# Moving transformed row-block pairs in the feed-forward, one more such pair in each head's gate and value product, and two subtractions written as one

## The chip, the cores and the metric

The kernel runs on one core of a Trainium2 chip. The metric is the device time in microseconds (us) of one execution. The kernel before has a median of 2198.53 us over three executions (2196.38 to 2199.3). A further execution was taken with the hardware profiler; every row of the profile below comes from that one.

## The reference, cut to what is computed

One layer with a sequence of 256 rows, a model width of 2048, 8 retention heads (key width 256, value width 512) and a feed-forward width of 5632. All inputs are float32.

```
h = rms_norm(x, g_mix[i])
proj = h @ w_in[i]
cb, cc, cv, q, k, v, g, gate_conv, gate_ret = jnp.split(proj, split_points, axis=-1)

y_conv = short_conv_mixer(cb, cc, cv, conv_w[i]) @ w_conv_out[i]
...
o = retention(q, k, v.reshape(bsz, s, RET_HEADS, RET_DV))
o = head_group_norm(o, g_ret[i], x.dtype)
y_ret = (jax.nn.silu(g) * o) @ w_ret_out[i]

merged = jax.nn.sigmoid(gate_conv) * y_conv + jax.nn.sigmoid(gate_ret) * y_ret
x = x + merged @ w_o[i]

h = rms_norm(x, g_ffn[i])
a, b = jnp.split(h @ w_ffn_in[i], 2, axis=-1)
x = x + (jax.nn.silu(a) * b) @ w_ffn_out[i]

ple_gate = jax.nn.sigmoid(rms_norm(x, g_ple[i]) @ w_ple_gate[i])
x = x + ple_gate * (p[i] @ w_ple_proj[i])
return rms_norm(x, g_final)
```

The change touches three kinds of product in it: the columns of `h @ w_in` that hold `g` and `v` of one head, the other double column blocks of `h @ w_in`, and `h @ w_ffn_in`.

## The kernel before

**How a product is formed.** Activations lie transposed in the on-chip memory, in blocks of 128 rows of the inner dimension, and weights stream in from HBM. Every float32 operand is used as two parts, hi (the value rounded to the matmul's input type) and lo (what is left of it). One block product is therefore three matmuls of 128x512: hi by hi, hi by lo, lo by hi. The function `thrice` issues them, and they are L230, L231 and L232 in the profile. For weights ScalarE (ACT) makes hi with a cast (L350) and VectorE (DVE) makes lo with a subtraction (L351); the matmul by a lo part cannot start before DVE has written it.

**Groups and places.** The function `product_group` multiplies the 256 rows by two weight blocks of 512 columns side by side, over an inner dimension of 16 row blocks. It takes the row blocks two at a time; these eight pairs are called places 0 to 7 here. A pair is a 2x2 block product (two row halves of the activations, two row blocks, two column blocks). A *plain* pair does it with 8 block products, 24 matmuls. A *transformed* pair uses the Winograd form of Strassen's scheme: 7 block products, 21 matmuls, and for it sums of weight blocks and sums of activation blocks. In the names, `b` is a weight block as loaded, `t` a weight sum, `h2T_s` or `hF_s` an activation sum and `h2T_d` or `hF_d` an activation difference, which plain pairs ahead of the last transformed one use.

**What a pair costs on the other engines.** A plain pair needs one ACT cast and one DVE subtraction of 128x2048. A transformed pair needs on DVE: the lo part of three weight blocks (128x1536, L351), four sums or differences of 128x512 in place in the raw tile (L278, L279, L281, L282), and the lo parts of the four sums (two of 128x1024, L285); on ACT a cast of 128x1536 (L350) and two of 128x1024 (L280, L283). The hi and lo parts come from one pool of 6 tiles (`part`): a plain pair takes 2 of them, a transformed pair 4. Raw weights have 3 tiles, which two loads of 512 KB each fill by SyncE's queue.

**The stages.** First the norm and head 0; then heads 1 to 7, each with a projection of q and k (`qk`), a gate and value group (`gv1` to `gv7`, a `product_group`) and the retention itself, and the output projection of the heads (`ro`) in between; then the convolution (groups `cv0` to `cv3`, `cb0`, `cb2`), the gates (groups `gate0` to `gate3`), `wo`, the feed-forward, the embedding gate and the final norm. The feed-forward runs over 11 groups `f0` to `f10`. Each ends with a sigmoid and four products on DVE (L830, L833) that give `f_ca`. After f2 to f9 come four chunks of 24 matmuls each of the product with `w_ffn_out` (`fo`, L370 to L372), two row block chunks for each of two column blocks; after f10 come the last twelve. The result of a group has to be transposed for that: `turn_a` does it with 8 small matmuls on TensorE (`aT`, L147).

**Which places are transformed.** In `gv`, `cv` and `cb` groups and in f0 and f1 places 1 and 3; in the gates places 1, 3 and 5; in f2 to f10 places 1, 3, 4 and 6.

**What sets the order.** Engines run their instructions in the order of their queues, which a scheduler fixes when the program is built. Work that must wait for other engines is put off by hand: `later(n, fn)` runs `fn` after n more groups, where a call of `group_done` after each pair or chunk counts one.

Of the kernel before, what the change touches and what calls it, by code (L numbers as in the profile page):

```python
# [950 lines left out]
```

## Time and profile before

| what | before |
|---|---|
| median of three executions | 2198.53 us (2196.38 to 2199.3) |
| the profiled execution | 2199.96 us, of which the span from first to last instruction is 2198.2 us |
| mean granted TensorE clock | 0.997 of full speed |
| TensorE, matmuls (PE) | busy 2169.9 us, 99% of the span, 9826 instructions |
| TensorE, weight loads (PEld, beside PE) | busy 1787.4 us, 81% |
| VectorE (DVE) | busy 1651.3 us, 75%, 1692 instructions |
| ScalarE (ACT) | busy 1062.8 us, 48%, 967 instructions |

A busy share is the part of the span in which the engine had an instruction in it. Matmuls overlap: a row gives about 0.39 us for one of 128x512, while in a run without waits a new one starts every 0.23 us. So the distance between starts, and not the duration in a row, is what a matmul takes from the time. In rows of the timeline "x2" is two equal instructions in a row, and the bracket at the end is the idle time of the engine just before, with the instruction that ended it.

### The profile page before, as it was taken

The numbers are of one execution on the slowest core, as the hardware profiler recorded it, in microseconds if no ns is written. First come the engines' busy times: TensorE is split into PE (matmuls) and PEld (weight loads), VectorE is DVE, ScalarE is ACT, GpSimd is POOL, SyncE is SP. The second block draws the span as 40 slices with busy tenths as digits, with TensorE's granted clock in tenths as the row PEclk, the third lists the DMA queues.
The fourth block names the chain that finished last, engine by engine and source line by source line (L and its number), as shares of the span: only waits on it lengthen the run. The fifth ranks groups of instructions, "written<-read, shape, count | busy, mean of one in ns | idle before, by whom it ended". The sixth has DMA issues, their size and how long they took to land.

```text
span 2198.2 us, 25135 instructions
## 1 busy us (share of the span) xinstructions
PE 2169.9 (99%) x9826; PEld 1787.4 (81%) x9826; DVE 1651.3 (75%) x1692; ACT 1062.8 (48%) x967; POOL 9.4 (0%) x19
## 2 busy tenths in 40 slices
PE   8999999999999999999999999999999999999998
PEld 7888888888888888888878888778777878777887
DVE  6687877467785468888987556888888888888555
ACT  6454544444544345555554345544545444445544
POOL 0000000000000000000000000000000000000000
PEclk9999999999999999999999999999999999999999
DMA  7555556655656665455657565456565555556553
GB/s 262 176 195 181 168 176 212 212 173 195 211 177 212 223 215 188 163 182 191 245 183 243 191 206 179 171 190 203 195 217 192 182 181 192 198 204 215 173 196 130
DMA packets 236024, 428.49 MB, mean 195 GB/s; under 512 B 12289, under 2 KB 47233, under 8 KB 235905
## 3 DMA queue, kind: packets, MB, share of 16 engines
q1 hardware_dynamic: 235904, 426.89, 57.8%
q8 instruction: 77, 1.26, 0.2%
q14 instruction: 43, 0.34, 0.0%
HBM read 420.54 MB, written 6.29 MB: 194 GB/s over the span
## 4 chain that ended last, share of the span: by engine, by line
PE 92%; DVE 4%; ACT 2%; issue 1%; DMA 1%; SPq 0%; ACTq 0%; POOLq 0%; DVEq 0%
PE f_p L231 6%; PE f_p L232 6%; PE f_p L230 6%; PE gv_p L230 4%; PE gv_p L231 4%; PE gv_p L232 4%; PE fo_ps L370 3%; PE fo_ps L372 3%; PE fo_ps L371 3%; PE qk_ps L372 3%; PE qk_ps L370 3%; PE qk_ps L371 3%; PE ro_ps L232 3%; PE ro_ps L230 3%; PE ro_ps L231 3%; PE cv_p L231 2%
## 5 line engine op out<-in xcount | busy, mean ns | idle before, releaser
L351 DVE TENSOR_TENSOR f_b_lo<-f_raw,f_b_hi 128x2048 fp32r<-128x2048 f32 (+1 forms) x88 | 179.2, 2046 | 66.7 <-ACT f_b_hi L350 66.7
L350 ACT CAST f_b_hi<-f_raw 128x2048 fp32r<-128x2048 f32 (+1 forms) x88 | 150.6, 1714 | 90.8 <-PE fo_ps L371 39.9
L231 PE MATMUL f_p<-f_b_lo,h2T_hi 128*128 128x512 f32 x402 | 157.1, 391 | 0.5 <-DVE f_b_lo L351 0.5
L232 PE MATMUL f_p<-f_b_hi,h2T_lo 128*128 128x512 f32 x402 | 156.5, 390 | 0.0
L350 ACT CAST gv_b_hi<-gv_raw 128x2048 fp32r<-128x2048 f32 (+1 forms) x56 | 101.0, 1805 | 101.6 <-PE qk_ps L371 45.4
L230 PE MATMUL f_p<-f_b_hi,h2T_hi 128*128 128x512 f32 x402 | 144.6, 393 | 4.1 <-ACT f_b_hi L350 4.1
L351 DVE TENSOR_TENSOR gv_b_lo<-gv_raw,gv_b_hi 128x2048 fp32r<-128x2048 f32 (+1 forms) x56 | 120.1, 2154 | 34.6 <-ACT gv_b_hi L350 34.6
L351 DVE TENSOR_TENSOR ro_lo<-ro_raw,ro_hi 128x2048 fp32r<-128x2048 f32 x32 | 73.4, 2293 | 88.5 <-ACT ro_hi L350 88.5
L371 PE MATMUL fo_ps<-fo_lo,aT_hi 128*128 128x512 f32 x352 | 137.9, 392 | 0.0
L370 PE MATMUL fo_ps<-fo_hi,aT_hi 128*128 128x512 f32 x352 | 137.1, 394 | 0.0
L372 PE MATMUL fo_ps<-fo_hi,aT_lo 128*128 128x512 f32 x352 | 137.0, 390 | 0.0
L231 PE MATMUL gv_p<-gv_b_lo,hT_hi 128*128 128x512 f32 x336 | 131.0, 390 | 0.0
L232 PE MATMUL gv_p<-gv_b_hi,hT_lo 128*128 128x512 f32 x336 | 130.8, 389 | 0.0
L230 PE MATMUL gv_p<-gv_b_hi,hT_hi 128*128 128x512 f32 x336 | 126.8, 393 | 0.0
L350 ACT CAST fo_hi<-fo_raw 128x2048 fp32r<-128x2048 f32 x44 | 84.2, 1914 | 69.1 <-PE fo_ps L371 38.8
L351 DVE TENSOR_TENSOR qk_lo<-qk_raw,qk_hi 128x2048 fp32r<-128x2048 f32 x32 | 73.3, 2291 | 58.5 <-ACT qk_hi L350 58.5
L280 ACT CAST f_t_hi<-f_raw 128x1024 fp32r<-128x1024 f32 x40 | 42.1, 1054 | 145.3 <-DVE f_raw L279 64.1
L351 DVE TENSOR_TENSOR fo_lo<-fo_raw,fo_hi 128x2048 fp32r<-128x2048 f32 x44 | 100.6, 2286 | 14.8 <-ACT fo_hi L350 14.8
L350 ACT CAST ro_hi<-ro_raw 128x2048 fp32r<-128x2048 f32 x32 | 61.2, 1912 | 99.5 <-PE ro_ps L231 65.8
L285 DVE TENSOR_TENSOR f_t_lo<-f_raw,f_t_hi 128x1024 fp32r<-128x1024 f32 x80 | 96.7, 1221 | 16.1 <-ACT f_t_hi L283 8.9
L371 PE MATMUL qk_ps<-qk_lo,hT_hi 128*128 128x512 f32 x256 | 100.3, 392 | 0.0
L372 PE MATMUL qk_ps<-qk_hi,hT_lo 128*128 128x512 f32 x256 | 99.8, 390 | 0.0
(459 smaller groups left out, 5751.0 us busy)
## 6 DMA issues: line engine op xcount, KB each, us to landing
f_raw<-in_w_ffn_in_dram SPq DMA_DIRECT2D x176, 512.0 KB, 4.5
gv_raw<-in_w_in_dram SPq DMA_DIRECT2D x112, 512.0 KB, 4.6
fo_raw<-in_w_ffn_out_dram SPq DMA_DIRECT2D x44, 1024.0 KB, 5.2
qk_raw<-in_w_in_dram SPq DMA_DIRECT2D x64, 512.0 KB, 4.6
ro_raw<-in_w_ret_out_dram SPq DMA_DIRECT2D x64, 512.0 KB, 4.7
cv_raw<-in_w_in_dram SPq DMA_DIRECT2D x64, 512.0 KB, 4.6
gate_raw<-in_w_in_dram SPq DMA_DIRECT2D x64, 512.0 KB, 4.8
cb_raw<-in_w_in_dram SPq DMA_DIRECT2D x32, 512.0 KB, 4.6
```

Source lines behind the costliest of these rows:

```text
L230: nc.tensor.matmul(out=ps, lhsT=xh, rhs=wh, start=first, stop=False)
L231: nc.tensor.matmul(out=ps, lhsT=xh, rhs=wl, start=False, stop=False)
L232: nc.tensor.matmul(out=ps, lhsT=xl, rhs=wh, start=False, stop=last)
L280: nc.scalar.copy(out=hi[:, 0:2, :], in_=raw[:, 0:2, :])
L285: tt(out=lo[:, js, :], in0=raw[:, js, :], in1=hi[:, js, :].bitcast(F32), op=ALU.subtract)
L350: last_copy[0] = nc.scalar.copy(out=hi[:, :n, :], in_=src)
L351: nc.vector.tensor_tensor(out=lo[:, :n, :], in0=src, in1=hi[:, :n, :].bitcast(F32), op=ALU.subtract)
L370: nc.tensor.matmul(out=ps, lhsT=xh[:, ts], rhs=wh, start=first, stop=False)
L371: nc.tensor.matmul(out=ps, lhsT=xh[:, ts], rhs=wl, start=False, stop=False)
L372: nc.tensor.matmul(out=ps, lhsT=xl[:, ts], rhs=wh, start=False, stop=last)
```

## The change

It does four things. The places become an argument: a tuple of the transformed places, and a string of forms by which the activation sums (S), differences (D) or nothing (-) are prepared.

1. Each of the seven groups `gv1` to `gv7` has a third transformed pair, at place 5.
2. In the feed-forward the transformed places are 0, 2, 4, 6 in f2 to f10 (before 1, 3, 4, 6), and 0, 2 in f0 and f1 (before 1, 3). The number of them stays.
3. In every transformed pair the two subtractions L278 and L279, each of 128x512, become one instruction of 128x2x512 (L284 in the kernel after), whose output rows are in reverse order and whose second operand is one block read twice.
4. `turn_a` is put off by three groups and not two, for all but the last group.

The groups `cv`, `cb` and `gate` keep their places. The arguments `k0` and `order` keep their defaults.

```
-FAST3 = (False, True, False, True, False, True, False, False)
-FAST2 = (False, True, False, True, False, False, False, False)
-FAST4 = (False, True, False, True, True, False, True, False)
+FORMS_MIX, FORMS_FFN = "DSDSDS--", "SDSDSDS-"
...
-    def product_group(lhs, forms, fast, w, c1, c2, name):
+    def product_group(lhs, forms, fast, w, c1, c2, name, k0=0, order=range(8)):
-        last_fast = max(i for i, f in enumerate(fast) if f)
+        last_fast = max(at for at, i in enumerate(order) if i in fast)
...
-        for i, f in enumerate(fast):
-            rows = w[2 * i * P : 2 * (i + 1) * P, :].rearrange("(c p) n -> p c n", p=P)
+        for at, i in enumerate(order):
+            f = i in fast
+            k = k0 + 2 * i
+            rows = w[k * P : (k + 2) * P, :].rearrange("(c p) n -> p c n", p=P)
...
-                tt(out=raw[:, 1, :], in0=raw[:, 1, :], in1=raw[:, 0, :], op=ALU.subtract)
-                tt(out=raw[:, 0, :], in0=raw[:, 3, :], in1=raw[:, 0, :], op=ALU.subtract)
+                b12 = raw[:, 0:1, :].broadcast_to([P, 2, W])
+                tt(out=raw[:, 1::-1, :], in0=raw[:, 1:4:2, :], in1=b12, op=ALU.subtract)
...
-        g, v = product_group(hT, hF, FAST2, w_in[0], C_RG + h * DV, C_RV + h * DV, f"gv{h}")
+        g, v = product_group(hT, hF, (1, 3, 5), w_in[0], C_RG + h * DV, C_RV + h * DV, f"gv{h}")
...
-        a, b = product_group(h2T, h2F, FAST4 if n > 1 else FAST2, w_ffn_in[0], n * W, D_FF + n * W, f"f{n}")
+        a, b = product_group(h2T, h2F, (0, 2, 4, 6) if n > 1 else (0, 2), w_ffn_in[0], n * W, D_FF + n * W, f"f{n}")
...
-        later(2, partial(turn_a, n, a))
+        later(3 if n < NF - 1 else 2, partial(turn_a, n, a))
```

How this moves instructions is shown at three places, by the order of one engine's queue. A row is the line, the operation, the output, the inputs and the shape; the number at the end of a name tells tiles apart.

VectorE in the middle of group f5, before: places 3 and 4 are both transformed, and place 5 is plain.

```order
L281 TENSOR_TENSOR f5_raw3_11874<-f5_raw3_11874 128x512
L282 TENSOR_TENSOR f5_raw3_11874<-f5_raw3_11874 128x512
L285 TENSOR_TENSOR f5_t3_lo_11882<-f5_raw3_11874,f5_t3_hi_11881 128x1024 x2
L351 TENSOR_TENSOR f5_b4_lo_11916<-f5_raw4_11912,f5_b4_hi_11915 128x1536
L278 TENSOR_TENSOR f5_raw4_11912<-f5_raw4_11912 128x512
L279 TENSOR_TENSOR f5_raw4_11912<-f5_raw4_11912 128x512
L281 TENSOR_TENSOR f5_raw4_11912<-f5_raw4_11912 128x512
L282 TENSOR_TENSOR f5_raw4_11912<-f5_raw4_11912 128x512
L285 TENSOR_TENSOR f5_t4_lo_11920<-f5_raw4_11912,f5_t4_hi_11919 128x1024
L351 TENSOR_TENSOR f5_b5_lo_11954<-f5_raw5_11950,f5_b5_hi_11953 128x2048
L285 TENSOR_TENSOR f5_t4_lo_11920<-f5_raw4_11912,f5_t4_hi_11919 128x1024
L351 TENSOR_TENSOR f5_b6_lo_11985<-f5_raw6_11981,f5_b6_hi_11984 128x1536
```

And the same stretch after:

```order
L356 TENSOR_TENSOR f5_b3_lo_11873<-f5_raw3_11869,f5_b3_hi_11872 128x2048
L356 TENSOR_TENSOR f5_b4_lo_11904<-f5_raw4_11900,f5_b4_hi_11903 128x1536
L284 TENSOR_TENSOR f5_raw4_11900<-f5_raw4_11900 128x2x512
L286 TENSOR_TENSOR f5_raw4_11900<-f5_raw4_11900 128x512
L287 TENSOR_TENSOR f5_raw4_11900<-f5_raw4_11900 128x512
L290 TENSOR_TENSOR f5_t4_lo_11908<-f5_raw4_11900,f5_t4_hi_11907 128x1024 x2
L356 TENSOR_TENSOR f5_b5_lo_11941<-f5_raw5_11937,f5_b5_hi_11940 128x2048
L356 TENSOR_TENSOR f5_b6_lo_11972<-f5_raw6_11968,f5_b6_hi_11971 128x1536
L284 TENSOR_TENSOR f5_raw6_11968<-f5_raw6_11968 128x2x512
L286 TENSOR_TENSOR f5_raw6_11968<-f5_raw6_11968 128x512
```

Between two transformed pairs there now stands a plain pair with its one instruction (`f5_b3_lo`, `f5_b5_lo`), and in this stretch no lo part of one pair's sums comes behind the lo part of the next pair any more.

TensorE in the feed-forward, before, at the end of the second `fo` chunk behind group f4; `aT4` is the transposed result of f4, and `f4_ca` its source.

```order
L370 MATMUL fo2_0_ps1_11622<-fo3_0_hi_11655,aT3_hi_11237 128x512
L371 MATMUL fo2_0_ps1_11622<-fo3_0_lo_11656,aT3_hi_11237 128x512
L372 MATMUL fo2_0_ps1_11622<-fo3_0_hi_11655,aT3_lo_11238 128x512
L147 MATMUL aT4_t0_11685<-ident_82,f4_ca_11319 128x128 x2
L147 MATMUL aT4_t2_11692<-ident_82,f4_ca_11319 128x128 x2
L370 MATMUL fo2_1_ps0_11701<-fo2_1_hi_11705,aT2_hi_10791 128x512
L371 MATMUL fo2_1_ps0_11701<-fo2_1_lo_11706,aT2_hi_10791 128x512
L372 MATMUL fo2_1_ps0_11701<-fo2_1_hi_11705,aT2_lo_10792 128x512
```

And after, at the transposes:

```order
L375 MATMUL fo2_1_ps1_11676<-fo2_1_hi_11679,aT2_hi_10823 128x512
L376 MATMUL fo2_1_ps1_11676<-fo2_1_lo_11680,aT2_hi_10823 128x512
L377 MATMUL fo2_1_ps1_11676<-fo2_1_hi_11679,aT2_lo_10824 128x512
L146 MATMUL aT4_t0_11709<-ident_82,f4_ca_11313 128x128 x4
L146 MATMUL aT4_t2_11716<-ident_82,f4_ca_11313 128x128 x4
L375 MATMUL fo2_1_ps0_11675<-fo3_1_hi_11725,aT3_hi_11265 128x512
L376 MATMUL fo2_1_ps0_11675<-fo3_1_lo_11726,aT3_hi_11265 128x512
L377 MATMUL fo2_1_ps0_11675<-fo3_1_hi_11725,aT3_lo_11266 128x512
```

The transposes of `aT4` now stand one chunk of 24 matmuls later, between the third and the fourth chunk.

VectorE in group gv3 behind its second transformed pair, before:

```order
L351 TENSOR_TENSOR gv3_b4_lo_2158<-gv3_raw4_2154,gv3_b4_hi_2157 128x2048
L167 TENSOR_TENSOR qkT3_lo_2065<-qkT3_t2_2073,qkT3_hi_2064 128x512
L311 TENSOR_TENSOR gv3_cb_1987<-gv3_p6_2057,gv3_ca_1986 128x512
L351 TENSOR_TENSOR gv3_b5_lo_2209<-gv3_raw5_2205,gv3_b5_hi_2208 128x2048
L312 TENSOR_TENSOR gv3_ca_1986<-gv3_p7_2050,gv3_cb_1987 128x512
L351 TENSOR_TENSOR gv3_b6_lo_2240<-gv3_raw6_2236,gv3_b6_hi_2239 128x2048
L313 TENSOR_TENSOR gv3_cb_1987<-gv3_p5_2003,gv3_ca_1986 128x512
L314 TENSOR_TENSOR gv3_cb_1987<-gv3_p5_2003,gv3_cb_1987 128x512
L510 TENSOR_TENSOR pr3_2199<-sc3_2186,mask3_1793 128x384
L351 TENSOR_TENSOR gv3_b7_lo_2271<-gv3_raw7_2267,gv3_b7_hi_2270 128x2048
```

And after:

```order
L356 TENSOR_TENSOR gv3_b5_lo_2209<-gv3_raw5_2205,gv3_b5_hi_2208 128x1536
L166 TENSOR_TENSOR qkT3_lo_2072<-qkT3_t2_2080,qkT3_hi_2071 128x512
L284 TENSOR_TENSOR gv3_raw5_2205<-gv3_raw5_2205 128x2x512
L286 TENSOR_TENSOR gv3_raw5_2205<-gv3_raw5_2205 128x512
L287 TENSOR_TENSOR gv3_raw5_2205<-gv3_raw5_2205 128x512
L290 TENSOR_TENSOR gv3_t5_lo_2213<-gv3_raw5_2205,gv3_t5_hi_2212 128x1024
L356 TENSOR_TENSOR gv3_b6_lo_2251<-gv3_raw6_2247,gv3_b6_hi_2250 128x2048
L515 TENSOR_TENSOR pr3_2199<-sc3_2186,mask3_1801 128x384
L290 TENSOR_TENSOR gv3_t5_lo_2213<-gv3_raw5_2205,gv3_t5_hi_2212 128x1024
L356 TENSOR_TENSOR gv3_b7_lo_2283<-gv3_raw7_2279,gv3_b7_hi_2282 128x2048
L519 TENSOR_TENSOR pl3_2201<-pr3_2199,ph3_2200 128x384
L316 TENSOR_TENSOR gv3_cb_1995<-gv3_p6_2064,gv3_ca_1994 128x512
```

Place 5 now has six instructions (128x1536, 128x2x512, two of 128x512, two of 128x1024) where one of 128x2048 stood, and the four that fold the matmul banks (L311 to L314 before, L316 to L319 after) have moved behind all of them.

## Rows read from the trace of the kernel before

**Rows 1.** Page, part 1 (busy us, share, instructions) and part 4 (ending chain).

```profile
PE 2169.9 (99%) x9826; PEld 1787.4 (81%) x9826; DVE 1651.3 (75%) x1692; ACT 1062.8 (48%) x967; POOL 9.4 (0%) x19
...
PE 92%; DVE 4%; ACT 2%; issue 1%; DMA 1%; SPq 0%; ACTq 0%; POOLq 0%; DVEq 0%
```

**Rows 2.** Busy us of each engine in stretches of 200 us; clock; DMA.

```profile
core 0: us, PE busy (x) PEld busy (x) DVE busy (x) ACT busy (x) POOL busy (x), PEclk, DMA share, GB/s
200.00:400.00 200.00, 200.00 (x918) 165.99 (x917) 150.41 (x168) 94.84 (x83) 2.07 (x3) 1.00 0.58 193
...
600.00:800.00 200.00, 200.00 (x900) 165.78 (x899) 120.22 (x113) 85.59 (x66) 1.38 (x2) 1.00 0.60 200
...
1000.00:1200.00 200.00, 199.18 (x877) 162.17 (x877) 169.90 (x158) 107.11 (x90) 0.00 (x0) 1.00 0.62 212
...
1600.00:1800.00 200.00, 197.21 (x872) 160.42 (x871) 171.20 (x165) 96.67 (x76) 0.00 (x0) 1.00 0.57 192
```

**Rows 3.** TensorE by line, 200 to 800 us: busy, mean ns; idle before.

```profile
L231 PE MATMUL gv_p<-gv_b_lo,hT_hi 128*128 128x512 f32 x272 | 106.0, 390 | 0.0
```

**Rows 4.** TensorE's timeline, a run without waits: first row and last.

```profile
1519.12 0.39 PE L230 MATMUL f_p<-f_b_hi,h2T_hi 128*128 128x512 f32 x1
...
1539.52 0.62 PE L230 MATMUL f_p<-f_b_hi,h2T_hi 128*128 128x512 f32 x2
```

**Rows 5.** Busy us by stretch, seven feed-forward periods: sum, and mean of one.

```profile
sum 457.45, PE 450.80 PEld 366.48 DVE 392.01 ACT 222.09 POOL 0.00; mean PE 64.40 PEld 52.35 DVE 56.00 ACT 31.73 POOL 0.00
```

**Rows 6.** TensorE's timeline, feed-forward: the instructions that waited, and four transposes.

```profile
1507.22 0.66 PE L147 MATMUL aT_t<-ident,f_ca 128*128 128x128 f32 x4 [0.49 <-DVE f_ca L833]
...
1513.42 0.60 PE L147 MATMUL aT_t<-ident,f_ca 128*128 128x128 f32 x4
1513.77 0.48 PE L371 MATMUL fo_ps<-fo_lo,aT_hi 128*128 128x512 f32 x1
1514.09 0.40 PE L372 MATMUL fo_ps<-fo_hi,aT_lo 128*128 128x512 f32 x1
...
1542.37 0.50 PE L231 MATMUL f_p<-f_t_lo,h2T_s 128*128 128x512 f32 x1 [0.19 <-DVE f_t_lo L285]
...
1545.08 0.50 PE L230 MATMUL f_p<-f_b_hi,h2T_hi 128*128 128x512 f32 x1 [0.38 <-ACT f_b_hi L350]
...
1999.82 0.50 PE L231 MATMUL f_p<-f_t_lo,h2T_s 128*128 128x512 f32 x1 [0.20 <-DVE f_t_lo L285]
```

**Rows 7.** TensorE by line, 1460 to 2060 us: the lines that waited.

```profile
L230 PE MATMUL f_p<-f_b_hi,h2T_hi 128*128 128x512 f32 x298 | 107.1, 393 | 3.3 <-ACT f_b_hi L350 3.3
L231 PE MATMUL f_p<-f_t_lo,h2T_s 128*128 128x512 f32 x108 | 43.1, 399 | 2.3 <-DVE f_t_lo L285 2.3
...
L147 PE MATMUL aT_t<-ident,f_ca 128*128 128x128 f32 x80 | 12.5, 278 | 3.2 <-DVE f_ca L833 3.2
```

**Rows 8.** VectorE by line and shape, whole span: busy, mean ns; idle before.

```profile
L351 DVE TENSOR_TENSOR f_b_lo<-f_raw,f_b_hi 128x2048 fp32r<-128x2048 f32 x48 | 109.8, 2290 | 29.3 <-ACT f_b_hi L350 29.3
...
L351 DVE TENSOR_TENSOR f_b_lo<-f_raw,f_b_hi 128x1536 fp32r<-128x1536 f32 x40 | 70.2, 1755 | 37.4 <-ACT f_b_hi L350 37.4
...
L285 DVE TENSOR_TENSOR f_t_lo<-f_raw,f_t_hi 128x1024 fp32r<-128x1024 f32 x80 | 96.7, 1221 | 16.1 <-ACT f_t_hi L283 8.9 <-ACT f_t_hi L280 6.5 <-PE f_p L232 0.7
...
L278 DVE TENSOR_TENSOR f_raw<-f_raw 128x512 f32<-128x512 f32 x40 | 27.5, 688 | 0.9
...
L598 DVE SCALAR_TENSOR_TENSOR ab<-qk_ps,r_r,rope_sb 128x512 f32<-128x512 f32 x32 | 22.4, 742 | 0.3 <-PE qk_ps L372 0.3
...
L830 DVE SCALAR_TENSOR_TENSOR f_ca<-f_ca,r_r,sa 128x512 f32<-128x512 f32 x22 | 16.3, 743 | 0.0
...
L562 DVE TENSOR_TENSOR on<-on,gv_ca 128x1024 f32<-128x1024 f32 x7 | 8.5, 1219 | 0.0
```

**Rows 9.** TensorE by line, 1000 to 1175 us, the gates: lines that waited.

```profile
L231 PE MATMUL gate_p<-gate_t_lo,hF_s 128*128 128x512 f32 x36 | 14.2, 395 | 0.5 <-DVE gate_t_lo L285 0.5
...
L230 PE MATMUL gate_p<-gate_t_hi,hF_s 128*128 128x512 f32 x36 | 11.8, 396 | 0.3 <-ACT gate_t_hi L283 0.3
```

More of the change, by code (lines that the diff above doesn't have):

```diff
@@ L163, in transposed_split @@
             pt = transposed(src, j0, f"{name}_t{j0}")
-            a = form_source(f"{name}_{j0}") if forms is not None and any(forms[1][len(forms[0]) :]) else None
+            a = form_source(f"{name}_{j0}") if forms is not None and forms[1][len(forms[0])] != "-" else None
             if gain is None:
@@ L199, in block_kernel, with further_forms @@
     t1, t2 = slice(0, P), slice(P, 2 * P)
-    def further_forms(a, forms, fast, name):
-        i = len(forms)
-        if not any(fast[i:]):
+    def further_forms(a, forms, kinds, name):
+        kind = kinds[len(forms)]
+        if kind == "-":
             forms.append(None)
@@ L208, in further_forms @@
         tt = nc.vector.tensor_tensor
-        n = 4 if fast[i] else 2
+        n = 4 if kind == "S" else 2
         mix = small.tile([P, 4, P], F32, tag="form_m", name=f"{name}_m", bufs=1)[:, :n, :]
-        if fast[i]:
+        if kind == "S":
             a11, a12, a21, a22 = a[:, 0, t1], a[:, 1, t1], a[:, 0, t2], a[:, 1, t2]
@@ L246, in plain_group @@
         return ps
-    def product_group(lhs, forms, fast, w, c1, c2, name):
-        last_fast = max(i for i, f in enumerate(fast) if f)
+    def product_group(lhs, forms, fast, w, c1, c2, name, k0=0, order=range(8)):
+        last_fast = max(at for at, i in enumerate(order) if i in fast)
         left = {p: 0 for p in range(1, 9)}
-        for i, f in enumerate(fast):
-            for p in (1, 2, 3, 4, 5, 6, 7) if f else (2, 4, 3, 5) if i < last_fast else (2, 4, 3, 8):
+        for at, i in enumerate(order):
+            f = i in fast
+            for p in (1, 2, 3, 4, 5, 6, 7) if f else (2, 4, 3, 5) if at < last_fast else (2, 4, 3, 8):
                 left[p] += 1 if f else 2
@@ L265, in product_group @@
         cb = blk([P, NT, W], F32, f"{name}_cb")
-        for i, f in enumerate(fast):
-            rows = w[2 * i * P : 2 * (i + 1) * P, :].rearrange("(c p) n -> p c n", p=P)
+        for at, i in enumerate(order):
+            f = i in fast
+            k = k0 + 2 * i
+            rows = w[k * P : (k + 2) * P, :].rearrange("(c p) n -> p c n", p=P)
             raw = raw_pool.tile([P, 4, W], F32, tag="raw", name=f"{name}_raw{i}")
@@ L271, in product_group @@
             nc.sync.dma_start(out=raw[:, 0:4:3, :], in_=rows[:, :, c2 : c2 + W])
-            blocks = lhs[2 * i : 2 * i + 2]
+            blocks = lhs[k : k + 2]
             (a11, a21), (a12, a22) = ([(h[:, t], l[:, t]) for t in (t1, t2)] for h, l in blocks)
@@ L302, in product_group @@
                     add(4, x2, b1)
-                    if i < last_fast:
+                    if at < last_fast:
                         add(5, x2, b2)
@@ L308, in product_group @@
                         add(8, x2, b2)
-            if i == last_fast:
+            if at == last_fast:
                 nc.scalar.copy(out=ca[:, 0, :], in_=banks[1])
@@ L314, in product_group @@
                 tt(out=cb[:, 0, :], in0=banks[5], in1=cb[:, 0, :], op=ALU.add)
-            if i < len(fast) - 1:
+            if at < len(order) - 1:
                 group_done()
@@ L590, in make_hF @@
                     )
-                further_forms(a, hF, FAST3, f"hF{n}_{j0}")
+                further_forms(a, hF, FORMS_MIX, f"hF{n}_{j0}")
     def rope(h, ps):
@@ L811, in block_kernel @@
             x1.append(xn)
-            later(1 + i, partial(turn_x, n + i, xn, rows2, G_FFN, h2T, "h2T", (h2F, FAST4)))
+            later(1 + i, partial(turn_x, n + i, xn, rows2, G_FFN, h2T, "h2T", (h2F, FORMS_FFN)))
     aT = {}
```

8 lines of the change are left out of this document (4 added, 4 removed).

## The prediction

> **What bounds the kernel now.** I read the page first. TensorE (PE) is in work for 99% of the span and has 92% of the chain that ended last; VectorE (DVE) is next with 75% [rows 1]. As a share is an average over stages, I then read busy time in stretches of 200 us, and there the reader is to see three kinds of stage [rows 2]. From 200 to 800 us, the heads, PE is busy without a gap, and DVE only for 150 us at their start and 120 at their end. In the gates (1000 to 1200 us) PE has 0.8 us without work, DVE 170 us of work. In the feed-forward (1600 to 1800 us is a typical stretch) PE lacks 2.8 us in 200, and DVE works 171 us. The granted clock is 1.00 throughout, so the clock has no part in it.
>
> In the heads nothing holds PE up: the `gv` matmuls have 0.0 us of idle time before them [rows 3]. So the heads are shortened by fewer matmuls only. The price of a matmul is not its 390 ns, since matmuls overlap, but the distance between starts. In a run without waits, 90 matmuls lie between the first row and the last, 1539.52 - 1519.12 = 20.40 us, thus 226.7 ns each [rows 4].
>
> For the feed-forward I looked for a period. The same matmul, waiting for the same instruction, stands at 1542.37 and at 1999.82 us, seven groups apart [rows 6], which gives 457.45 / 7 = 65.35 us [rows 5]. The work of one period is 4 x 21 + 4 x 24 = 180 matmuls of the group and 4 x 24 = 96 of `fo`: 276 x 0.2267 = 62.57 us. The transposes are two blocks of four small matmuls. A block that did not wait takes 1513.77 - 1513.42 = 0.35 us, and the matmul behind it is followed after 0.32 us and not 0.23 [rows 6], so 0.44 us, and 0.87 us for both. 62.57 + 0.87 = 63.44, so **1.91 us are lost in each period**. The timeline shows where [rows 6]: 0.19 us for `f_t_lo` and 0.38 us for `f_b_hi`, both behind place 4, and 0.49 us for `f_ca` ahead of the transposes. Over the whole stretch these lines have all the idle time, 3.3 + 2.3 + 3.2 = 8.8 us [rows 7]; the rest of the loss is that matmuls start late around a wait (their pipeline has to fill).
>
> **Why PE waits behind place 4.** A transformed pair costs DVE 1755 + 4 x 688 + 2 x 1221 ns = 6.95 us, a plain one 2.29 us [rows 8], while PE works on them for 21 x 0.2267 = 4.76 and 24 x 0.2267 = 5.44 us. Two transformed pairs in a row take 13.9 us from DVE and 9.5 us from PE: DVE falls 4.4 us behind. A lead cannot be stored up, since two such pairs want 8 of the 6 `part` tiles. The order of before shows the effect, the second `f5_t4_lo` stands behind `f5_b5_lo`, and PE waits for this lo part and for the cast of the next pair [rows 6].
>
> **The change, part by part.**
>
> *Third transformed pair in gv1 to gv7.* It removes 7 x 3 = 21 matmuls: -21 x 0.2267 = **-4.76 us**. On DVE it puts 6.95 (or 6.8 with the joined instruction) in place of 2.29: +4.5 us per head, 31.6 us over seven. It lies beside PE's work: in two of the three stretches alone DVE has 49.6 + 79.8 = 129 us without work [rows 2]. Inside a group the tightest sequence becomes transformed, plain, transformed, plain, transformed: per two pairs 9.1 us on DVE for 10.2 on PE, and 6 `part` tiles, so DVE is not overtaken. The gates already run three transformed pairs at these places and idle for 0.5 + 0.3 us in the stretch that holds nearly all of the four groups [rows 9]. Without that cover the price would be 0 to 4.5 us per head; I take 0, and 1 us in all as an allowance in the range.
>
> The Trainium skill, "TensorE: Matmul & The Clock Gate", section "Back-to-back issue gap", gives about 131 ns as the sustained spacing of 512-column matmuls in a real kernel, and some 216 ns for a lone one. The trace disagrees, with 226.7 ns over 90 of them [rows 4]. By the page the 21 matmuls would be worth an estimated 2.75 us instead of 4.76. The sum goes by the row.
>
> *Places 0, 2, 4, 6 in f2 to f10.* No two transformed pairs stand side by side: 10.2 us of PE against 9.1 of DVE per two pairs and 6 tiles. That takes away the cause of the waits behind place 4. What is late next? Place 0 now asks for 6.8 us of DVE work at once where 2.29 did. Its cover is the stretch in which PE works on place 7 and on `fo`: 5.44 + 4 x 5.44 + 0.87 = 28.1 us. In it DVE has 14 instructions of 128x512 (4 that fold banks, 4 that finish the group, 4 that add `fo`, 2 lo parts of `aT`) at 0.688, 4 products at 0.743, 4 lo parts of `fo` at 2.29, and place 0's 6.8: 28.6 us by the durations [rows 8]. Durations overstate it: by them a period of before is 58.7 us, and the busy time of a period is 56.0 [rows 5], a factor of 0.954. That makes 27.2 us, enough with 0.9 us to spare, and the lo parts of place 0's sums are wanted only 9 and 15 matmuls (2.0 and 3.4 us) after its start. This is the tightest place of the change.
>
> *`turn_a` later by a chunk.* The transposes move behind the third chunk, 24 x 0.2267 = 5.44 us later, and their wait was 0.49 us: it goes, with 5 us to spare. `aT4` is first multiplied two groups on (the `fo` chunks behind f4 and f5 use `aT2` and `aT3`), so nothing waits for it. Its two lo parts on DVE move nearer to place 0's work; they are in the 27.2 us. No DMA moves.
>
> Of the 1.91 us I let 1.75 go and leave 0.16 for what the transposes cost around them. Nine groups (f2 to f10; f10's transposes stay where they are, some 0.5 us of it, within the rounding): 9 x 1.75 = **-15.75 us**. Bounds: nothing, if the waits only move; 9 x 1.91 = 17.2 us if all goes.
>
> *f0 and f1 from places 1, 3 to 0, 2.* The same work two pairs apart in both; one pair earlier asks DVE sooner at the start, when the norm's work is still there. No row prices it; I take **0**, from -2 to +2 us.
>
> *One subtraction of 128x2x512 for two of 128x512.* 83 of them (76 transformed pairs before and 7 new). The trace has no reversed output. Nearest rows: DVE takes 1219 ns for 128x1024, against 2 x 688 for two of 512, so 0.16 us less; an operand that is read from a broadcast costs nothing (L598 742 ns, L830 743 with plain operands) [rows 8]. DVE is hidden in all stages, so I take **0**; bounds: -1 us (a wait at the gates that shrinks), +2 us if it ran at twice 1219 ns.
>
> **Sum.** -4.76 - 15.75 + 0 + 0 = -20.5 us, from the profiled 2199.96 us: 2179.5. The profiled execution is 1.4 us above the median of the three runs, 2198.53, so an unprofiled run should lie at or a little under that: I say **2179 us**.
>
> **The rivals.**
>
> A. *The feed-forward's waits move to place 0.* If DVE enters the stretch some 4 to 5 us behind, or the order makes it wait inside, the 0.9 us and the 3.4 us are used up and PE waits 1 to 1.75 us at each group's start; of 15.75 us 0 to 7 are kept: 2179.5 + 9 to 15.75 = 2188 to 2195. For it: 56.0 us of DVE work in a period of 65.35 is 86%, and the order lets nothing overtake. Against it: the joined subtraction takes 0.64 us off each period, and the alternation gives DVE 1.1 us per two pairs before it enters place 7.
>
> B. *Slower: the heads become bound by DVE.* Place: gv1 to gv7, pairs 4 to 7. There the casts and the lo parts of three transformed pairs meet the retention's small steps (`qkT3_lo`, `pr3`, `pl3` in the order above) in a fixed queue. If each head loses more than 20.5 / 7 = 2.9 us beyond its saving, the gain is gone; at the full 4.5 us it is 31.6 - 20.5 = 11 us slower, 2210. Against it: 129 us without work [rows 2] and the gates' 0.8 us.
>
> C. *The reversed, broadcast subtraction is slow.* A period after has 56.0 - 4 x 0.16 = 55.4 us of DVE work in 63.6, so the instruction would have to take over 1.22 + 8.2 / 4 = 3.3 us, 2.7 times its nearest row, before DVE sets the period; then the feed-forward's gain goes by 36 us for each us more (9 x 4 pairs). Half of that price would already cost some of it: 2182 to 2195. Rows 8 show nothing near it.
>
> D. *PE's matmuls are not the bound where they are removed.* The weight loads' 81% might count instead, or DMA. Then the 21 matmuls are worth nothing: 2199.96 - 15.75 = 2184. Against it: PE's 200.00 of 200 us and the even 226.7 ns. The Trainium skill, "Perfetto Trace Analysis", section "Identifying the Most-Contended Engine", calls matmul busy share a poor measure of headroom and goes by the weight loads' share. By it PE has 19% in hand here, and the trace does not bear that out for the heads, where matmuls start at an even distance and none waits.
>
> That the change doesn't do what it says is excluded: the order has 21 matmuls fewer in `gv`.
>
> **How the numbers follow.** My forecast (2174 to 2185) 0.72; A 0.13; B 0.05; C 0.03; D 0.05; 0.02 for what I have not seen. The range reaches from 2170 (all of 17.2, -2 for f0 and f1, -1 at the gates, and the median's lower side) to 2191, half way into A. 0.2%, about 4.4 us, is what a measurement can tell here. Faster: all of the forecast and D, nearly all of A and half of C, 0.91; same: A's end and a weak B, 0.05; slower: 0.04.
>
> **What would show it.** Right: in the feed-forward no idle time before `f_t_lo`, `f_b_hi` and `aT`, and a period of about 63.6 us; `gv` matmuls 1281 with 0.0 us idle; DVE's work in the heads up by some 4.5 us for each `gv` group. Wrong: PE waits at place 0 for `f_b_lo` or `f_t_lo` or at the `aT` banks (A); idle time in front of `gv_p` (B); the L284 row well above 1.3 us (C).

## The result, and the profile after

The kernel after takes 2178.24 us (median of four runs, 2177.72 to 2179.43), the kernel before 2198.91 us (four runs). The ratio is 0.9906, with a 95% interval of 0.9894 to 0.9917: 20.7 us faster. The forecast was 2179 us. The profiled execution has 2179.43 us and a span of 2177.6 us, 20.6 us less than before.

The sum came out almost exactly, but three of its terms did not. I read the same views as before. First the page, parts 1 and 4 [rows 1]:

```profile
PE 2157.6 (99%) x9805; PEld 1788.8 (82%) x9805; DVE 1676.3 (77%) x1651; ACT 1075.1 (49%) x981; POOL 9.4 (0%) x19
...
PE 98%; ACT 1%; DMA 0%; DVE 0%; issue 0%; SPq 0%; ACTq 0%; POOLq 0%
```

The 21 matmuls are gone, VectorE has 25 us more work, and its share of the ending chain fell from 4% to nothing. Then the busy time in the stretches of 200 us [rows 2], with that of 1200 to 1400 us, where f0 lies:

```profile
200.00:400.00 200.00, 200.00 (x918) 165.96 (x917) 165.38 (x181) 99.94 (x91) 2.07 (x3) 1.00 0.60 198
...
600.00:800.00 200.00, 200.00 (x901) 165.90 (x900) 126.24 (x109) 86.05 (x68) 0.69 (x1) 1.00 0.61 201
...
1000.00:1200.00 200.00, 199.42 (x880) 162.74 (x879) 167.41 (x146) 106.30 (x90) 0.00 (x0) 1.00 0.61 210
1200.00:1400.00 200.00, 195.65 (x883) 161.92 (x883) 124.57 (x126) 92.52 (x100) 0.69 (x1) 0.98 0.56 184
...
1600.00:1800.00 200.00, 200.00 (x896) 165.84 (x895) 176.48 (x157) 100.79 (x79) 0.00 (x0) 1.00 0.60 200
```

The feed-forward has no gap left. In the heads VectorE went up by 15 us in the first stretch and TensorE still has none. New is 1200 to 1400 us: 4.35 us without work, and a clock of 0.98. Before had 0.61 us without work there and a clock of 1.00:

```profile
1200.00:1400.00 200.00, 199.39 (x911) 165.09 (x910) 123.42 (x126) 91.38 (x101) 0.69 (x1) 1.00 0.59 193
```

To see which stage gave what, the first start of one matmul per stage is enough. The view by tile has it ("first to last start"). Of before:

```profile
L230 PE MATMUL gv_p<-gv_b_hi,hT_hi x336: 389/389/480, 109.7 to 657.5; 128*128 128x512 f32 x168
...
L230 PE MATMUL cv_p<-cv_b_hi,hT_hi x192: 388/389/481, 791.9 to 966.6; 128*128 128x512 f32 x192
...
L230 PE MATMUL gate_p<-gate_b_hi,hT_hi x160: 387/389/496, 1010.9 to 1181.3; 128*128 128x512 f32 x160
...
L230 PE MATMUL f_p<-f_b_hi,h2T_hi x402: 387/389/504, 1361.5 to 2018.3; 128*128 128x512 f32 x134
...
L370 PE MATMUL pg_ps<-pg_hi,h3T_hi x96: 389/389/473, 2088.5 to 2159.4; 128*128 128x512 f32 x96
```

And of after:

```profile
L229 PE MATMUL gv_p<-gv_b_hi,hT_hi x280: 387/389/481, 110.5 to 654.0; 128*128 128x512 f32 x140
...
L229 PE MATMUL cv_p<-cv_b_hi,hT_hi x192: 389/389/476, 787.9 to 960.8; 128*128 128x512 f32 x192
...
L229 PE MATMUL gate_p<-gate_b_hi,hT_hi x160: 388/389/481, 1004.7 to 1174.4; 128*128 128x512 f32 x160
...
L229 PE MATMUL f_p<-f_b_hi,h2T_hi x406: 387/389/796, 1354.7 to 1998.3; 128*128 128x512 f32 x136
...
L375 PE MATMUL pg_ps<-pg_hi,h3T_hi x96: 389/389/476, 2068.2 to 2139.1; 128*128 128x512 f32 x96
```

| from the first matmul of ... to that of ... | before | after | change |
|---|---|---|---|
| start to `gv` | 109.7 | 110.5 | +0.8 |
| `gv` to `cv` (heads) | 682.2 | 677.4 | -4.8 |
| `cv` to `gate` (convolution) | 219.0 | 216.8 | -2.2 |
| `gate` to `f` (gates, `wo`) | 350.6 | 350.0 | -0.6 |
| `f` to `pg` (feed-forward) | 727.0 | 713.5 | -13.5 |
| `pg` to the end of the span | 109.7 | 109.4 | -0.3 |

The period of the feed-forward is read from two equal instructions six groups apart, the transposes of `aT`, now eight in a row and without a wait [rows 6]:

```profile
1570.80 1.03 PE L146 MATMUL aT_t<-ident,f_ca 128*128 128x128 f32 x8
...
1951.62 1.03 PE L146 MATMUL aT_t<-ident,f_ca 128*128 128x128 f32 x8
```

380.82 / 6 = 63.47 us, where 63.44 was the bare work and 65.35 the period before. That is 1.88 us a group, 16.9 us over nine groups, and so more than the 13.5 us of the stage. Counted directly, f2 begins with the 373rd `f_p` matmul, which starts at 1451.70 us in before and at 1449.08 us in after. From there to the first `pg` matmul before takes 636.8 us and after 619.1, 17.6 us less; f0 and f1 take 90.2 us in before and 94.4 in after, 4.2 us more. The lines that waited in 1460 to 2060 us wait no more [rows 7]:

```profile
L229 PE MATMUL f_p<-f_b_hi,h2T_hi 128*128 128x512 f32 x297 | 102.9, 389 | 0.0
...
L230 PE MATMUL f_p<-f_t_lo,h2T_s 128*128 128x512 f32 x105 | 40.9, 389 | 0.0
...
L146 PE MATMUL aT_t<-ident,f_ca 128*128 128x128 f32 x78 | 10.6, 272 | 0.0
```

The 4.2 us are to be looked for at f0. TensorE's timeline there, in after:

```profile
1386.41 1.12 PE L146 MATMUL h2T_t<-ident,x 128*128 128x128 f32 x4 [2.98 <-ACT h2T_a L182]
1388.89 0.80 PE L229 MATMUL f_p<-f_b_hi,h2T_hi 128*128 128x512 f32 x1 [1.36 <-ACT f_ca L315]
1389.48 0.63 PE L230 MATMUL f_p<-f_b_lo,h2T_hi 128*128 128x512 f32 x1
1389.91 0.63 PE L231 MATMUL f_p<-f_b_hi,h2T_lo 128*128 128x512 f32 x1
```

and the same stretch by busy time and clock:

```profile
1386.00:1388.80 2.80, 1.12 (x4) 0.72 (x4) 1.66 (x5) 1.79 (x4) 0.00 (x0) 0.55 0.00 0
1388.80:1393.00 4.20, 4.11 (x10) 3.24 (x11) 3.22 (x6) 2.08 (x3) 0.00 (x0) 0.50 0.01 2
```

The second four transposes of the last block of activations wait 2.98 us, and a matmul of f0 waits 1.36 us for ScalarE's copy `f_ca` of a matmul bank. Behind that, matmuls start every 0.43 us and not 0.23: the granted clock is 0.50, the lower of its two levels (1.2 GHz), for some 4 us after the engine had stood still.

The joined subtraction takes what an ordinary one of 1024 elements takes [rows 8]:

```profile
L284 DVE TENSOR_TENSOR f_raw<-f_raw 128x1024 f32<-128x1024 f32 x40 | 49.0, 1225 | 1.3
```

### The profile page after: what moved, and what is told of

The parts are those of the page before. It is cut to its first block, busy times and chain, and to the rows that moved or that the text cites. A ratio compares the mean times of both kernels' runs of the same rounds, so it can differ in the third digit from the quotient of the medians.

```text
span 2177.6 us, 25125 instructions
## 1 busy us (share of the span) xinstructions
PE 2157.6 (99%) x9805; PEld 1788.8 (82%) x9805; DVE 1676.3 (77%) x1651; ACT 1075.1 (49%) x981; POOL 9.4 (0%) x19
## 4 chain that ended last, share of the span: by engine, by line
PE 98%; ACT 1%; DMA 0%; DVE 0%; issue 0%; SPq 0%; ACTq 0%; POOLq 0%
PE f_p L229 7%; PE f_p L230 7%; PE f_p L231 7%; PE gv_p L229 4%; PE gv_p L231 4%; PE gv_p L230 4%; PE fo_ps L375 4%; PE fo_ps L377 4%; PE fo_ps L376 4%; PE qk_ps L377 3%; PE qk_ps L375 3%; PE qk_ps L376 3%; PE ro_ps L230 3%; PE ro_ps L229 3%; PE ro_ps L231 3%; PE cv_p L230 3%
## 5 line engine op out<-in xcount | busy, mean ns | idle before, releaser
L356 DVE TENSOR_TENSOR f_b_lo<-f_raw,f_b_hi 128x1536 fp32r<-128x1536 f32 (+1 forms) x88 | 177.7, 2046 | 57.2 <-ACT f_b_hi L355 57.2
L355 ACT CAST f_b_hi<-f_raw 128x1536 fp32r<-128x1536 f32 (+1 forms) x88 | 149.2, 1717 | 91.1 <-PE fo_ps L376 26.5
L230 PE MATMUL gv_p<-gv_b_lo,hT_hi 128*128 128x512 f32 x280 | 109.1, 390 | 0.0
L231 PE MATMUL gv_p<-gv_b_hi,hT_lo 128*128 128x512 f32 x280 | 108.9, 390 | 0.0
L229 PE MATMUL gv_p<-gv_b_hi,hT_hi 128*128 128x512 f32 x280 | 102.2, 394 | 0.0
L231 PE MATMUL ro_ps<-ro_hi,yrT_lo 128*128 128x512 f32 x256 | 99.6, 389 | 0.0
```

What stands on the lines that cost most here:

```text
L229: nc.tensor.matmul(out=ps, lhsT=xh, rhs=wh, start=first, stop=False)
L230: nc.tensor.matmul(out=ps, lhsT=xh, rhs=wl, start=False, stop=False)
L231: nc.tensor.matmul(out=ps, lhsT=xl, rhs=wh, start=False, stop=last)
L355: last_copy[0] = nc.scalar.copy(out=hi[:, :n, :], in_=src)
L356: nc.vector.tensor_tensor(out=lo[:, :n, :], in0=src, in1=hi[:, :n, :].bitcast(F32), op=ALU.subtract)
```

## The experiments

Every run was timed beside the kernel before on the same chip, and the ratio is to that kernel. Its medians differ by up to 1.1 us between the rows below, so a difference between the medians of two rows is uncertain by about as much.

| run | what it is | median us | before there | ratio (95% interval) |
|---|---|---|---|---|
| after | all four parts | 2178.24 | 2198.91 | 0.9906 (0.9894 to 0.9917) |
| e1_gv | before + third pair in `gv` | 2194.78 | 2200.03 | 0.9976 (0.9967 to 0.9985) |
| e2_places | before + places in the feed-forward | 2185.13 | 2200.03 | 0.9930 (0.9917 to 0.9942) |
| e3_turn_a | before + later `turn_a` | 2194.66 | 2200.03 | 0.9975 (0.9966 to 0.9985) |
| e4_join | before + one subtraction for two | 2193.64 | 2200.03 | 0.9968 (0.9957 to 0.9980) |
| e5_f0 | after, f0 transformed at place 0 alone | 2172.30 | 2199.73 | 0.9875 (0.9862 to 0.9889) |
| e6_cv | after + third pair in `cv` | 2179.15 | 2199.73 | 0.9908 (0.9894 to 0.9921) |
| e7_dve1 | after + 1.22 us of VectorE per pair | 2180.63 | 2199.73 | 0.9917 (0.9903 to 0.9930) |
| e8_dve2 | after + 2.44 us of VectorE per pair | 2219.75 | 2199.73 | 1.0091 (1.0077 to 1.0104) |
| e9_split | after, two subtractions again | 2180.82 | 2199.81 | 0.9913 (0.9899 to 0.9926) |
| e10_turn_a2 | after, `turn_a` as before | 2178.71 | 2199.81 | 0.9905 (0.9892 to 0.9919) |
| e11_f0f1 | e5, and f1 at places 0, 2, 4, 6 | 2174.96 | 2199.81 | 0.9886 (0.9873 to 0.9900) |

### One part alone: e1, e2, e3, e4

**The third pair in `gv`.**

```diff
-        g, v = product_group(hT, hF, FAST2, w_in[0], C_RG + h * DV, C_RV + h * DV, f"gv{h}")
+        g, v = product_group(hT, hF, FAST3, w_in[0], C_RG + h * DV, C_RV + h * DV, f"gv{h}")
```

> The kernel before with one part of the change alone: a third transformed pair, at place 5, in gv1 to gv7. Theory (TensorE sets the heads' time, VectorE's added work is hidden): 21 matmuls at 226.7 ns, 4.8 us faster, 0.0 us idle before the gv matmuls. Rival (VectorE becomes the bound in the heads): less than 2 us faster, or slower, with idle time in front of gv_p.

5.2 us faster. TensorE by line, 200 to 800 us:

```profile
L231 PE MATMUL gv_p<-gv_b_lo,hT_hi 128*128 128x512 f32 x224 | 87.4, 390 | 0.0
```

No idle time, and the heads (`gv` to `cv`) last 677.4 us in its trace as in after's, 4.8 us less than before: 229 ns for each of the 21 matmuls. VectorE's added work is hidden.

**The places in the feed-forward.** The code of after with `(1, 3)` in `gv`, `later(2, ...)` for `turn_a` and two subtractions, so only this is new, with the forms that go with it:

```diff
-        a, b = product_group(h2T, h2F, FAST4 if n > 1 else FAST2, w_ffn_in[0], n * W, D_FF + n * W, f"f{n}")
+        a, b = product_group(h2T, h2F, (0, 2, 4, 6) if n > 1 else (0, 2), w_ffn_in[0], n * W, D_FF + n * W, f"f{n}")
```

> The kernel before with one part alone: transformed pairs at places 0, 2, 4, 6 in f2 to f10 and 0, 2 in f0 and f1. VectorE has the same work as before. Theory (the waits behind place 4 come from two transformed pairs side by side): these waits go, some 1.1 us in each of nine groups, 10 us, the waits before the aT transposes stay, and the new wait around f0 that the trace of after shows costs 4 us: 5 to 7 us faster. Rival (the waits come from VectorE's mean load of 86%): they only move to another place, and the time is that of before or up to 4 us above.

14.9 us faster, more than twice what I expected. TensorE by line, 1455 to 2060 us:

```profile
L229 PE MATMUL f_p<-f_b_hi,h2T_hi 128*128 128x512 f32 x304 | 105.5, 390 | 0.0
...
L230 PE MATMUL f_p<-f_t_lo,h2T_s 128*128 128x512 f32 x108 | 42.0, 389 | 0.0
...
L146 PE MATMUL aT_t<-ident,f_ca 128*128 128x128 f32 x80 | 12.1, 271 | 0.0
```

The reader is to see the last line: the transposes do not wait either, though `turn_a` comes as early as before. VectorE has the same work here as before (1692 instructions in both), so its mean load did not make the waits; the neighbourhood of places 3 and 4 did. Whether two neighbours want too much of VectorE's time or too many of the 6 `part` tiles, this run does not separate. And VectorE, no longer behind, has `f_ca` ready in time. The waits at f0 are in this trace too, 1.58 us for `h2T_a` and 1.56 us for `f_ca`.

**The later transposes.**

```diff
-        later(2, partial(turn_a, n, a))
+        later(3 if n < NF - 1 else 2, partial(turn_a, n, a))
```

> The kernel before with one part alone: turn_a put off by three groups and not two. Theory: the wait before the transposes of aT2 to aT9 goes, about 0.65 us in each of eight groups with the late starts behind it: 5 us faster, and the waits behind place 4 stay. Rival (the moved transposes push the lo parts of aT into the work of the next group): the wait moves to the next group and nothing is won, 0 to 1 us.

5.4 us faster, as expected: the transposes' idle time in 1455 to 2020 us is 0.0, and the two waits behind place 4 keep their 3.3 and 2.3 us. The part does what it says when it is alone; e2 removes the same wait in another way.

**One subtraction for two.**

```diff
-                tt(out=raw[:, 1, :], in0=raw[:, 1, :], in1=raw[:, 0, :], op=ALU.subtract)
-                tt(out=raw[:, 0, :], in0=raw[:, 3, :], in1=raw[:, 0, :], op=ALU.subtract)
+                b12 = raw[:, 0:1, :].broadcast_to([P, 2, W])
+                tt(out=raw[:, 1::-1, :], in0=raw[:, 1:4:2, :], in1=b12, op=ALU.subtract)
```

> The kernel before with one part alone: the two subtractions of 128x512 as one of 128x2x512. Theory as predicted (VectorE is hidden where PE does not wait for it): the instruction takes 1.22 us, the time is that of before or 1 us less. Rival (VectorE's length matters wherever PE waits for a lo part): the waits in the cv groups and gates (2.4 + 0.9 us less in the trace of after) and part of those behind place 4 go, 3 to 8 us faster.

6.4 us faster: the rival. By first starts, `cv` to `gate` is 216.8 us (219.0 before), `gate` to `f` 349.5 (350.6), `f` to `pg` 724.2 (727.0). The 1.1 us from `gate` to `f` are not the instruction's: e1 and e3, with two subtractions, take 349.7 us there. The largest single wait that went is one of 1.22 us in the convolution of before, here with VectorE's instructions ahead of it:

```profile
900.39 2.28 DVE L351 TENSOR_TENSOR cv_b_lo<-cv_raw,cv_b_hi 128x2048 fp32r<-128x2048 f32 x1
902.59 1.22 DVE L285 TENSOR_TENSOR cv_t_lo<-cv_raw,cv_t_hi 128x1024 fp32r<-128x1024 f32 x1
904.85 0.69 DVE L731 TENSOR_TENSOR y<-bT,y 128x512 f32<-128x512 f32 x1 [1.04 <-PE bT L147]
908.08 0.69 DVE L311 TENSOR_TENSOR cv_cb<-cv_p,cv_ca 128x512 f32<-128x512 f32 x1 [2.54 <-PE cv_p L232]
...
911.68 4.48 DVE L351 TENSOR_TENSOR cv_b_lo<-cv_raw,cv_b_hi 128x2048 fp32r<-128x2048 f32 x2
```

```profile
914.02 0.50 PE L231 MATMUL cv_p<-cv_b_lo,hT_hi 128*128 128x512 f32 x1 [1.22 <-DVE cv_b_lo L351]
```

and the same place in e4_join:

```profile
898.94 1.22 DVE L285 TENSOR_TENSOR cv_t_lo<-cv_raw,cv_t_hi 128x1024 fp32r<-128x1024 f32 x1
900.07 0.68 DVE L731 TENSOR_TENSOR y<-bT,y 128x512 f32<-128x512 f32 x1
900.67 2.28 DVE L351 TENSOR_TENSOR cv_b_lo<-cv_raw,cv_b_hi 128x2048 fp32r<-128x2048 f32 x1
904.32 0.69 DVE L311 TENSOR_TENSOR cv_cb<-cv_p,cv_ca 128x512 f32<-128x512 f32 x1 [1.36 <-PE cv_p L232]
...
908.04 4.48 DVE L351 TENSOR_TENSOR cv_b_lo<-cv_raw,cv_b_hi 128x2048 fp32r<-128x2048 f32 x2
```

What changed is the order. In before the last lo part of the pair's sums (`cv_t_lo`) stands behind the `cv_b_lo` of two later pairs, in e4 behind that of one. So TensorE finishes the transformed pair late in before, VectorE idles 2.54 us for it (the 1.04 us are for a transpose), and the next `cv_b_lo` are late in turn. The joined instruction is all that differs between the two programs, so the scheduler's other order comes from it; the 0.16 us that it saves is no measure of that. This is shown for the one place alone. In the feed-forward, where the waits for `f_t_lo` went from 2.3 us to 1.0, order and shorter work are not separated.

### Around f0: e5 and e11

```diff
-        a, b = product_group(h2T, h2F, (0, 2, 4, 6) if n > 1 else (0, 2), w_ffn_in[0], n * W, D_FF + n * W, f"f{n}")
+        a, b = product_group(h2T, h2F, (0, 2, 4, 6) if n > 1 else (0, 2) if n else (0,), w_ffn_in[0], n * W, D_FF + n * W, f"f{n}")
```

> The kernel after with one pair less: group f0 has a transformed pair at place 0 alone, not at 0 and 2, which costs 3 matmuls, 0.68 us. Theory: the new waits around f0 in after (2.98 us of the second half of the last h2T transposes on ACT's h2T_a, 1.36 us on ACT's f_ca, and nine matmuls at the half clock behind them) come from matmul banks: a transformed pair holds seven of the eight until the copy f_ca behind the last one. With the last one at place 0 they come free some 10 us sooner: the waits go, 4 to 7 us less, 0.7 us more, so 2172 to 2175. Rival (the norm's work on ACT and DVE is late, whatever the banks): the waits stay, 2178 to 2180.

2172.30 us: 5.9 us less than after's median, with three matmuls more. No matmul of its feed-forward waits any more, all four blocks of transposes of the last activations run by 1370.97 us instead of 1386.41, and the clock stays up:

```profile
1383.00:1388.80 5.80, 5.80 (x27) 4.83 (x26) 3.77 (x5) 2.79 (x4) 0.00 (x0) 1.00 0.58 190
1388.80:1393.00 4.20, 4.20 (x21) 3.46 (x20) 3.01 (x3) 1.09 (x1) 0.00 (x0) 1.00 0.64 232
```

`f` to `pg` is 707.1 us here against 713.5, so the waits and the low clock cost after 6.4 + 0.7 = 7.1 us. A transformed pair writes seven banks (p1 to p7 in `product_group`) of the eight, and they are held until the copy and the additions behind the last transformed pair; the transposes of the last activations have one bank between them. That fits both waits of after, which end with the reading of such a bank. During the 2.98 us ScalarE and VectorE read the first four transposes out of the bank in turn, from 1383.46 to 1386.35 us, and both had stood idle just before (2.52 and 2.58 us), so their load did not make the wait.

How long the banks are held is set by ScalarE's queue. The last matmul of f0's place 2 and the copy that frees the first bank, in after:

```profile
1373.53 0.39 PE L231 MATMUL f_p<-f_t_hi,h2T_lo 128*128 128x512 f32 x1
...
1388.26 0.58 ACT L315 COPY f_ca<-f_p 128x512 f32<-128x512 f32 x1
```

and the copy and the last block of transposes in e5_f0:

```profile
1357.27 0.57 ACT L315 COPY f_ca<-f_p 128x512 f32<-128x512 f32 x1
...
1370.97 0.60 PE L146 MATMUL h2T_t<-ident,x 128*128 128x128 f32 x4
```

In after the copy comes 14.7 us behind the pair's last matmul, since eleven other ScalarE instructions stand ahead of it, eight of them reads of the very transposes that want a bank. In e5_f0 it comes 31 us earlier than in after, and not the some 10 us that I had reckoned with. So e5 shows what the waits cost; it does not separate the place of the last transformed pair from the other order of ScalarE's queue, nor from the 4.5 us of VectorE's work that it takes out of f0.

```diff
-        a, b = product_group(h2T, h2F, (0, 2, 4, 6) if n > 1 else (0, 2), w_ffn_in[0], n * W, D_FF + n * W, f"f{n}")
+        a, b = product_group(h2T, h2F, (0, 2, 4, 6) if n else (0,), w_ffn_in[0], n * W, D_FF + n * W, f"f{n}")
```

> The kernel after with group f0 transformed at place 0 alone and f1 at places 0, 2, 4, 6 as f2 to f10: 3 matmuls more and 6 less. Theory (f1 has alternating pairs and all banks, so VectorE keeps up without the fo phase): the run with f0 alone less 6 x 0.2267 = 1.4 us, 2170 to 2172. Rival (f1 has no fo phase ahead of it to hide place 0's lo parts, and its pairs 4 and 6 find VectorE late): waits in f1, the time of the run with f0 alone or up to 3 us above.

2174.96 us, 2.7 us above e5: the rival. The intervals of the two ratios overlap, but in the traces `f` to `pg` is 710.2 us against 707.1. TensorE by line, 1430 to 1475 us:

```profile
L229 PE MATMUL f_p<-f_b_hi,h2T_hi 128*128 128x512 f32 x33 | 12.8, 407 | 1.3 <-ACT f_b_hi L355 1.2
...
L230 PE MATMUL f_p<-f_t_lo,h2T_s 128*128 128x512 f32 x12 | 4.8, 399 | 0.5 <-DVE f_t_lo L290 0.5
```

These waits lie in f2, which now follows a full f1 without a `fo` phase between. My reading, which no run tests further, is that 10.2 us of TensorE against 9.1 of VectorE per two pairs is too thin to run on from group to group, once the folding and the products at a group's end come on top; f1 with two transformed pairs, as in after, leaves the room.

### How much room VectorE has: e7 and e8

In f2 to f10 each transformed pair writes the lo parts of its first two sums twice (e7), or all four (e8). The second writing puts the same values in the same place.

```diff
-                for js in (slice(0, 2), slice(2, 4)):
+                twice = name[0] == "f" and int(name[1:]) > 1
+                for js in (slice(0, 2),) * (1 + twice) + (slice(2, 4),):
```

> The kernel after with added work on VectorE: in f2 to f10 each transformed pair writes the lo parts of its first two sums twice, 1.22 us more, 4.9 us in a period of 63.4 (36 instructions, 44 us in all). Theory (DVE is covered by 0.9 to 3.4 us at place 0 and by 8 us over a period): at most 1 us per group slower, 0 to 9 us. Rival (DVE already sets the feed-forward's time): 30 to 44 us slower.

> The kernel after with twice that: in f2 to f10 all four lo parts of the sums are written twice, 2.44 us more for each transformed pair, 9.8 us in a period. Theory: DVE's work of a period comes to 56 + 9.8 = 66 us, over the 63.4 of TensorE, so the cover is gone: 20 to 45 us slower. Rival (DVE has more room than the busy time says): under 10 us slower.

e7 is 2.4 us slower than after by the medians for 44 us of added work, with ratios whose intervals overlap. From 1600 to 1800 us VectorE is busy 189.9 us, and TensorE has no gap:

```profile
1600.00:1800.00 200.00, 200.00 (x896) 165.83 (x895) 189.88 (x171) 101.11 (x80) 0.00 (x0) 1.00 0.57 200
```

The few waits in its feed-forward are at f2 and f3 (0.7 us in all). e8 adds another 44 us and is 39 us slower than e7. A period of it:

```profile
1521.33:1588.73 67.40, 66.50 (x285) 51.67 (x285) 64.42 (x59) 31.34 (x25) 0.00 (x0) 1.00 0.53 187
```

Now VectorE sets the period: 67.40 us, nine times 3.9 us above after's. So the room is between 4.9 and 9.8 us in a period, where 8 was worked out; if all that exceeds it counts in full, it is 9.8 - 3.9 = 5.9 us, less than the balance gave.

### The parts taken out of after: e9 and e10; and a group more: e6

e9_split is after with the two subtractions of before, e10_turn_a2 is after with `later(2, partial(turn_a, n, a))`.

> The kernel after with the two subtractions of 128x512 again as two instructions; places, gv and turn_a stay. Theory (the joined instruction changes VectorE's queue around the cv groups and gates, and VectorE's length is covered in the feed-forward): 2 to 4 us slower than after, 2180 to 2182, with the waits of cv and gates back and none in the feed-forward. Rival (it is needed to keep the feed-forward free of waits, 0.64 us a period): 6 us slower or more, 2184 and up.

> The kernel after with turn_a put off by two groups again. Theory (with places 0, 2, 4, 6 the result f_ca is ready early enough, as the run with the places alone has no wait before the transposes): the same time within 0.5 us. Rival (the prediction's step: the delay itself removes the wait): 4 to 5 us slower.

e9 is 2.6 us above after by the medians, with intervals that overlap (0.9899 to 0.9926 against 0.9894 to 0.9917); in its trace `cv` to `gate` is 219.2 us again, and `f` to `pg` 714.4 (after 713.5), with no wait in f2 to f10. The wait of 1.22 us before a `cv_b_lo` is back. `gate` to `f` is 349.7 us, no longer than after's 350.0, so the 0.6 us there do not come from the instruction. In after, then, the joined instruction is worth about 2 us in the convolution and the feed-forward does not need it. e10 is the same as after: the later `turn_a` adds nothing to the places.

```diff
-        c, v = product_group(hT, hF, (1, 3), w_in[0], C_C + n * W, C_V + n * W, f"cv{n}")
+        c, v = product_group(hT, hF, (1, 3, 5), w_in[0], C_C + n * W, C_V + n * W, f"cv{n}")
```

> The kernel after with a third transformed pair, at place 5, in the four cv groups too (cb as before): 12 matmuls less. Theory (DVE has 34 of 200 us without work in this stretch, and transformed and plain pairs alternate): 2.7 us faster. Rival (in the convolution the lo parts meet the products of the convolution on DVE, which is busy 166 of 200 us): new waits of 1 us or more in each cv group, the same time or slower.

The same time as after: the rival, though not in its size. `cv` to `gate` lasts 217.6 us by first starts (786.5 to 1004.1), where 216.8 less 12 matmuls would be 214.1; 3.5 us are lost. The rows name 0.5 us of it, before `cv_b_lo`; the rest are matmuls that start late around short waits, which no row prices one by one.

## Why the prediction was right, point by point

| term | predicted | measured |
|---|---|---|
| third pair in `gv` | -4.76 | -4.8 |
| f2 to f10, places and `turn_a` | -15.75 (0 to -17.2) | -17.6 |
| f0 and f1 | 0 (-2 to +2) | +4.2 |
| joined subtraction, outside the feed-forward | 0 (-1 to +2) | -2.2 (convolution) |
| gates and `wo`, not named | 0 | -0.6 |
| start and end, not named | 0 | +0.5 |
| sum against the span | -20.5 | -20.6 |

The terms measured add up to -20.5; the rest is rounding. The two rows before the sum are no more than what the traces scatter by: with the same instructions there, the start takes 108.1 us in e2 and 110.5 in after, and `gate` to `f` 349.6 us in e8 and 351.5 in e10.

**What held.** A matmul is worth the distance between starts: 4.8 us for 21, in e1 and in after. The 131 ns, weighed in the prediction (the Trainium skill, "TensorE: Matmul & The Clock Gate", "Back-to-back issue gap"), would have given an estimated 2.75 us; the heads do not bear it out. The waits behind place 4 came from the two neighbouring transformed pairs; e2 shows it with VectorE's work unchanged. The cover of place 0 was enough: the period is 63.47 us, and e7 and e8 hold the room between 4.9 and 9.8 us a period. Of the rivals, A (waits that move to place 0), B (heads bound by VectorE), C (a slow subtraction: 1225 ns) and D (matmuls that are worth nothing) did not come.

**What did not hold, and cancelled.** That the sum is right to 0.1 us is luck: f0 and f1, the joined subtraction and f2 to f10 all lie outside the bounds given for them, and their errors nearly cancel. First, the term for f0 and f1. I looked at VectorE's work there and not at the matmul banks. With pairs at places 0 and 2, seven of eight are taken from the group's first pair on and held until the copy behind the second, while the last activations still have to be transposed. This cost 7.1 us in after (e5), where before lost some 3 us in the same groups (90.2 us against 87.9 in e5, which has three matmuls more). Second, the joined subtraction: "hidden in all stages" was wrong by its own rows, which had waits of TensorE on VectorE in the gates [rows 9], as the convolution had too. I priced the instruction's duration; in the convolution, the one place looked into, what counted is the order that the scheduler makes of it (e4, -6.4 us alone; about -2 us in after, e9). Third, the split of the feed-forward's gain: I gave the transposes' share to `turn_a`. The places alone take all of it (e2), and `turn_a` takes the same 5 us only where the places are not changed (e3, e10).

**Why the parts do not add up.** Alone they give 5.2 + 14.9 + 5.4 + 6.4 = 31.9 us, together 20.7. All of e3's gain and e4's from f2 on (635.2 us to `pg` against 636.8, 1.6 us) are waits that e2 removes as well: some 7 us counted twice. The other 4 us are not settled one by one; the start of after is 0.8 us longer than before's, and f0's wait for `h2T_a` is longer in after (2.98 us) than in e2 and e9 (1.58 us), which have two subtractions.
